# Pool maps moved to a score-bank pair, and FFN squares queued behind the copies of a finished head pair, in a hybrid decoder layer on eight cores

## The chip, the cores and the metric

The kernel runs on the 8 NeuronCores of one Trainium2 chip. Each core computes half of one of four sequences, and no core talks to another. The metric is device time in microseconds of the slowest core. Executions fall into a fast state and a slow one, in which the cores of a die have a clearly lower granted TensorE clock (0.921 to 0.935 on cores 4 to 7 in the slow run of the changed kernel, 0.990 to 0.993 on the others); only fast executions are compared here. "Granted clock" is the share of full TensorE clock that the profile records.

Two kernels are compared, "before" and "the changed kernel". Time before: 1625.96 us (median of 3, 1623.55 to 1628.05).

## The reference, cut to what matters

The layer mixes tokens in three ways from one normalised input, projects, and runs a squared-ReLU MLP.

```python
proj = rmsnorm(x, g_mix) @ w_in                 # q, k, v | u (pooling) | qm (memory queries)
y_attn = dilated_window_attention(...)          # 8 heads of 64, three dilations merged
d = causal_multiscale_pool(u)                   # trailing means of 2/4/8/16 tokens, minus the token
y_pool = einsum('bsgc,gce->bsge', d, w_pool) * pool_scale      # the "pool maps"
y_mem = cross_attention(qm, memory)             # 4 heads
x = x + concat(y_attn, y_pool, y_mem) @ w_out
a = relu(rmsnorm(x, g_ffn) @ w_ff1)
x = x + (a * a) @ w_ff2                         # the "squares"
return rmsnorm(x, g_final)
```

## The kernel before

A core works through tiles of 512 tokens: four halo tiles (only keys, values and pooling margin) and eight own tiles. While the FFN of tile j runs as 64 TensorE groups of 8 matmuls each, the attention of tile j+1 is slipped in between the groups. The groups are FF1 half 0 (positions 0 to 15), FF2 half 0 (16 to 31), FF1 half 1 (32 to 47), FF2 half 1 (48 to 63). Work for between the groups is a list of (position, function).

PSUM is the memory that the matmuls write to. The kernel uses eight banks of it: two "mm" banks in turn for projections and FFN, two score pairs `sc` of two banks each, two banks `ob` for the attention output. In the listings below, `val` is what VectorE copies out of `ob`, `rt` what ScalarE's relu leaves for the square.

```python
mm  = [psum(f"mm{i}", [128, 512], F32) for i in range(2)]
scb = [psum(f"sc{i}", [128, 2, 512], F32) for i in range(2)]
ob  = [psum(f"ob{i}", [128, 512], F32) for i in range(2)]
rt  = [sb(f"rt{i}", [128, 16 + TOK], F32) for i in range(2)]   # relu results (and pooling sums)

def run(groups, side):
    side = sorted(side, key=lambda t: t[0])
    p = 0
    for s, g in enumerate(groups):
        while p < len(side) and side[p][0] <= s:
            side[p][1](); p += 1
        g()
    ...

def front(bt):      # scores of one batch for two heads -> sc pair; exp on ACT -> P; mask product on DVE
    ...
def back(bt):       # P times V -> ob[0], ob[1]; the first batch of a head pair overwrites ob
    ...
    if bt["post"] is None:
        return
    ch = bt["post"]                       # last batch of a head pair: take ob out
    for hh in range(2):
        lo, o2 = 64 * hh, 64 - 64 * hh
        T.op("act", ... den[lo:lo+64] = Ln(ob[hh][o2:o2+64]))
        T.op("dve", ... val[lo:lo+64] = copy(ob[hh][lo:lo+64]))
    T.op("act", ... den = Exp(-den))
    T.op("pool", ... yT[:, ch] = val * den)

def maps(ch):       # one pool map: one matmul into an mm bank, one scaled copy on ACT
    m_, bm_ = next_mm()
    mm_ops(m_[:].rearrange("p (r c) -> p r c", r=4), bm_,
           [(wpool[:, ch, :], dT[:, ch, :].rearrange("p (c r) -> p r c", r=4), [b_wp, b_dT])])
    T.op("act", ... yT[:, 4 + ch, :] = m_ * csm_t[:, 1 + ch:2 + ch])

def ff1(f_):        # 8 matmuls -> mm bank; relu on ACT -> rt; square on DVE -> aT
    def f():
        ...
        mm_ops(m_[:], bm_, [... for k in range(8)])
        r_, br_ = R[cnt["rt"] % len(R)]; cnt["rt"] += 1
        T.op("act", ... r_ = Relu(m_))
        def finish():
            ...
            T.op("dve", ... aT[:, f_ % 16, :] = r_ * r_)
        ...                                # (cut: the last tile keeps four of them back)
        finish()

# the schedule of tile j+1 beside the FFN of tile j
side += att_side(j + 1, 1.875, -4 if first else 0)
pst = pool_steps(j + 1)                    # 11 pooling steps, then the two maps
side += [(17 + i, f) for i, f in enumerate(pst[:-2])] + [(36.5, pst[-2]), (38.5, pst[-1])]
a2 = stage_A(j + 2)                        # RMS norm of tile j+2: squares, statistics, norms
side += ln_side(a2, 6.2, 2, 33.5, 35.2, 1.2)
```

The softmax here doesn't subtract the row's maximum and nothing guards it: scores larger than these inputs give would overflow.

Of the kernel before, what the change touches and what calls it, by code (L numbers as in the profile page):

```python
# [107 lines left out]
def build_nc(n_own=NOWN, races=False):  # L108
# [20 lines left out]
    with ExitStack() as es:  # L129
# [442 lines left out]
        def att_batches(j):  # L572
# [40 lines left out]
                        post=pr if dl == 4 else None))  # L613
            return batches

        def front(bt):
            si, pi = cnt["sc"] % 2, cnt["P"] % NPB
            cnt["sc"] += 1
            cnt["P"] += 1
            s_, bs_, P_, bP_ = scb[si], b_sc[si], Pbuf[pi], b_P[pi]  # L620
            n = len(bt["qk"])
            for i, (sec, l, r) in enumerate(bt["qk"]):
                for hh in range(2):
                    o2 = s_[:, hh, :] if sec is None else s_[:, hh, sec * 128:(sec + 1) * 128]
                    lo = 64 * hh
                    rr = r[lo:lo + 64]
                    if len(rr.shape) == 3:
                        o2 = o2.rearrange("p (a b) -> p a b", a=rr.shape[1])
                    T.op("pe", lambda: nc.tensor.matmul(o2, lhsT=l[lo:lo + 64], rhs=rr, start=True, stop=True),  # L629
                         reads=bt["qk_reads"], writes=[bs_], mark=(i == n - 1 and hh == 1))  # L630
            T.op("act", lambda: nc.scalar.activation(out=P_[:], in_=s_[:], func=AF.Exp, scale=0.125),  # L631
                 reads=[bs_], writes=[bP_])
            if bt["mask"] is not None:
                m, a = bt["mask"]
                Pv = P_[:].rearrange("p h (a q) -> p h a q", a=a)
                T.op("dve", lambda: nc.vector.tensor_tensor(out=Pv, in0=Pv, in1=m, op=ALU.mult),  # L636
                     reads=[bP_, b_E, b_E16], writes=[bP_])
            bt["P"] = (P_, bP_)

        def back(bt):  # L640
            P_, bP_ = bt["P"]
            n = len(bt["pv"])
            for hh in range(2):
                v0 = bt["v0"] + 64 * hh
                for i, (sec, l, oo) in enumerate(bt["pv"]):
                    if sec is None:
                        r_, o_ = P_[:, hh, :], ob[hh][:]
                    else:
                        r_ = P_[:, hh, sec * 128:(sec + 1) * 128]
                        o_ = ob[hh][:].rearrange("p (r c) -> p r c", r=4)[:, oo[0], oo[1]]  # L650
                        r_ = r_.rearrange("p (a b) -> p a b", a=o_.shape[1])
                    T.op("pe", lambda: nc.tensor.matmul(o_, lhsT=l[:, v0:v0 + 128], rhs=r_,  # L652
                                                        start=(bt["first"] and i == 0),
                                                        stop=(bt["last"] and i == n - 1), skip_group_check=True),
                         reads=bt["pv_reads"] + [bP_], writes=[b_ob[hh]], mark=(i == n - 1))
            if bt["post"] is None:
                return
            ch = bt["post"]
            for hh in range(2):
                lo, o2 = 64 * hh, 64 - 64 * hh  # L660
                T.op("act", lambda: nc.scalar.activation(out=den[lo:lo + 64, :], in_=ob[hh][o2:o2 + 64, :], func=AF.Ln),  # L661
                     reads=[b_ob[hh]], writes=[b_den[hh]])
                T.op("dve", lambda: nc.vector.tensor_copy(out=val[lo:lo + 64, :], in_=ob[hh][lo:lo + 64, :]),  # L663
                     reads=[b_ob[hh]], writes=[b_val[hh]])
            T.op("act", lambda: nc.scalar.activation(out=den[:], in_=den[:], func=AF.Exp, scale=-1.0),
                 reads=b_den, writes=b_den)
            T.op("pool", lambda: nc.gpsimd.tensor_tensor(out=yT[:, ch, :], in0=val[:], in1=den[:], op=ALU.mult),  # L667
                 reads=b_den + b_val, writes=[b_yT[ch]])


        def pool_steps(j):
            first_own = (j == NHALO)
            b_serial = Buf("serial")
            W = 16 + TOK
            S1, S2 = rt
            b_S1, b_S2 = b_rt
            ops = []

            def add(out, in0, in1, rd, wr):
                e = "pool" if first_own else "dve"  # L680
                ops.append(lambda: T.op(e, lambda: T.eng[e].tensor_tensor(out=out, in0=in0, in1=in1, op=ALU.add),
                                        reads=rd, writes=wr + ([b_serial] if first_own else [])))

            for ch in range(2):
                Uc = U[:, ch, :]
                add(S1[:, 1:W], Uc[:, 1:W], Uc[:, 0:W - 1], [b_U], [b_S1])
                if ch == 0:
                    add(S2[64:128, 3:W], S1[64:128, 3:W], S1[64:128, 1:W - 2], [b_S1], [b_S2])
                else:
                    add(S2[:, 3:W], S1[:, 3:W], S1[:, 1:W - 2], [b_S1], [b_S2])  # L690
                    add(S1[:, 7:W], S2[:, 7:W], S2[:, 3:W - 4], [b_S2], [b_S1])
                    add(S2[64:128, 15:W], S1[64:128, 15:W], S1[64:128, 7:W - 8], [b_S1], [b_S2])
                halves = ((S1, b_S1, 0), (S2, b_S2, 64))
                if first_own:
                    for s_, bs_, p0 in halves:
                        ops.append(lambda s_=s_, bs_=bs_, p0=p0, ch=ch: T.op(
                            "pool", lambda: nc.gpsimd.tensor_tensor(out=s_[p0:p0 + 64, 16:32], in0=s_[p0:p0 + 64, 16:32],
                                                                   in1=cpc_t[p0:p0 + 64, ch, :], op=ALU.mult),
                            reads=[b_g], writes=[bs_, b_serial]))
                inv = csm_t[:, 3 + ch:4 + ch]  # L700
                for s_, bs_, p0 in halves:
                    ops.append(lambda s_=s_, bs_=bs_, p0=p0, ch=ch, Uc=Uc, inv=inv: T.op(
                        "dve", lambda: nc.vector.scalar_tensor_tensor(out=dT[p0:p0 + 64, ch, :], in0=s_[p0:p0 + 64, 16:W],
                                                                      scalar=inv[p0:p0 + 64, :], in1=Uc[p0:p0 + 64, 16:W],
                                                                      op0=ALU.mult, op1=ALU.subtract),
                        reads=[bs_, b_U, b_g], writes=[b_dT]))
            ops.append(u_margin)

            def maps(ch):
                m_, bm_ = next_mm()  # L710
                mm_ops(m_[:].rearrange("p (r c) -> p r c", r=4), bm_,
                       [(wpool[:, ch, :], dT[:, ch, :].rearrange("p (c r) -> p r c", r=4), [b_wp, b_dT])])
                T.op("act", lambda: nc.scalar.activation(out=yT[:, 4 + ch, :], in_=m_[:], func=AF.Copy,
                                                         scale=csm_t[:, 1 + ch:2 + ch]),
                     reads=[bm_, b_g], writes=[b_yT[4 + ch]])

            ops += [lambda: maps(0), lambda: maps(1)]
            return ops

        def u_margin():  # L720
# [26 lines left out]
        def stage_K(j, late=None):  # L747
# [9 lines left out]
            def ff1(f_):  # L757
                def f():
# [19 lines left out]
                    if late is not None and f_ < 4:  # L778
                        st.setdefault("finish", []).append(finish)
                    else:  # L780
                        for g in st.pop("finish", []):
                            g()
                        finish()
                    if f_ % 4 == 3:
                        ring_issue()
                return f
# [30 lines left out]
# [5 lines that stand above are left out]
                while p < len(side) and side[p][0] <= s:  # L822
                    side[p][1]()
                    p += 1
                g()
            while p < len(side):
                side[p][1]()
                p += 1
# [130 lines left out]
        for j in range(NHALO, NT):  # L959
# [26 lines left out]
            if not last:  # L986
                side += att_side(j + 1, 1.875, -4 if first else 0)
                pst = pool_steps(j + 1)
                side += [(17 + i, f) for i, f in enumerate(pst[:-2])] + [(36.5, pst[-2]), (38.5, pst[-1])]
                if j + 2 < NT:  # L990
                    a2 = stage_A(j + 2)
                    side += ln_side(a2, 6.2, 2, 33.5, 35.2, 1.2)
                side += [(44, lambda j=j: load_x("pool", (j + 1) % 2, xr[j + 1 - NHALO]))]
# [128 lines left out]
```

## Time and profile before

| | before |
|---|---|
| time, median of 3 | 1625.96 us |
| span of the profiled execution, slowest core | 1638.0 us |
| TensorE / VectorE / ScalarE busy | 95% / 58% / 44% |
| tile period, fifth to seventh interval | 183.72, 183.68, 182.17 us |

The last row is worked out from the trace: the time from the first output-projection matmul of one own tile to that of the next. There are seven such intervals. The last three are the same on all eight cores within 0.04 us. The first four vary between cores by 3 to 19 us, because of loads and the granted clock.

The head of the profile page, the slowest core (engine, busy us, share of the span, instructions; PE is TensorE's matmuls, PEld its weight loads, DVE VectorE, ACT ScalarE, POOL GpSimd):

```profile
span 1638.0 us, 27926 instructions; the slowest of 8 cores (1605.7 to 1638.0 us)
...
PE 1558.9 (95%) x9722; PEld 755.0 (46%) x9722; DVE 944.4 (58%) x1378; ACT 722.9 (44%) x1085; POOL 161.1 (10%) x219
...
PEclk9998788999999999999999999999999999999998
```

TensorE (PE) is the bottleneck, so only its gaps matter. The clock row (one digit for each fortieth of the span, in tenths) has a 7 and three 8s in slices four to seven; core 3 was throttled between about 100 and 300 us (granted clock 0.80 from 150 to 250 us, where core 7 has 1.00), which makes it longer than most cores. So the table of TensorE's waits (who waited for whom: us in total, times, longest) is shown for core 3 and for core 7. Core 3:

```profile
PE mm L350 <- DVE acc L381: 24.2, 3, 17.7
PE mm L350 <- ACT rt L768: 12.7, 10, 4.6
PE ob L652 <- DVE val L663: 11.0, 29, 0.9
```

The same table of core 7, the two lines on the copies and on `rt`:

```profile
PE ob L652 <- DVE val L663: 12.2, 30, 1.4
PE mm L350 <- ACT rt L768: 8.3, 9, 4.2
```

The waits on `rt` and on `val` are what the change is about. The single waits behind such a sum are called idle entries below: idle time that the profile lists before an instruction, in square brackets, with what ended it. The timeline of core 3 shows one of each (columns: start us, duration us, engine, line, operation, out<-in, count, idle of that engine before and what ended it). First the copies, with TensorE, ScalarE (ACT) and VectorE (DVE) together, near the end of the second FF1 half:

```profile
1092.53 0.61 PE L652 MATMUL ob<-P,Vd 128*128 128x128 bf16 x8
...
1092.97 1.89 PE L350 MATMUL mm<-h2T,ring 128*128 128x512 bf16 x8
1093.52 1.21 ACT L661 ACTIVATE den<-ob 64x512 f32<-64x512 f32 x2
1093.60 0.69 DVE L775 TENSOR_TENSOR aT<-rt 128x512 bf16<-128x512 f32 x1 [1.03 <-ACT rt L768]
1094.32 1.41 DVE L663 COPY val<-ob 64x512 f32<-64x512 f32 x2
...
1095.15 0.38 PE L652 MATMUL ob<-P,Vd 128*128 128x128 bf16 x4 [0.29 <-DVE val L663]
...
1095.88 0.38 PE L652 MATMUL ob<-P,Vd 128*128 128x128 bf16 x4 [0.34 <-DVE val L663]
...
1096.10 1.89 PE L350 MATMUL mm<-aT,ring 128*128 128x512 bf16 x8
```

VectorE was idle for 1.03 us, then did a square that had been waiting for its relu, and only then the two copies, although `ob` was complete (ScalarE read it at 1093.52). TensorE had to wait before each half of the next head pair. Next the two pool maps, with TensorE and, of ScalarE, the two relus that free a bank:

```profile
1069.23 0.61 PE L350 MATMUL mm<-dT,wpool 128*128 128x512 bf16 x1
1069.60 0.60 ACT L768 ACTIVATE rt<-mm 128x512 f32<-128x512 f32 x1 [1.63 <-DVE hT L411]
1069.66 0.63 PE L652 MATMUL ob<-P,Vd 128*128 128x128 bf16 x8
1070.34 1.89 PE L350 MATMUL mm<-h2T,ring 128*128 128x512 bf16 x8
1072.16 0.64 PE L629 MATMUL sc<-Q,KT 64*128 64x128 bf16 x16
1072.73 1.90 PE L350 MATMUL mm<-h2T,ring 128*128 128x512 bf16 x8
1074.47 0.61 PE L350 MATMUL mm<-dT,wpool 128*128 128x512 bf16 x1
1074.84 0.60 ACT L768 ACTIVATE rt<-mm 128x512 f32<-128x512 f32 x1
1075.58 1.89 PE L350 MATMUL mm<-h2T,ring 128*128 128x512 bf16 x8 [0.50 <-ACT rt L768]
1077.30 0.61 PE L652 MATMUL ob<-P,Vd 128*128 128x128 bf16 x8
1077.75 1.89 PE L350 MATMUL mm<-h2T,ring 128*128 128x512 bf16 x8
```

After the second map the next FF1 group needs the mm bank of the group before the map, whose relu has just been issued: 0.50 us of idle.

### The profile page before, as it was taken

How to read it: one execution, taken by the hardware profiler on the slowest of the kernel's cores; microseconds unless marked ns; L12 is line 12 of the kernel's file. 1: busy time of each engine (PE TensorE's matmuls, PEld its weight loads, DVE VectorE, ACT ScalarE, POOL GpSimd, SP SyncE). 2: the span in 40 equal slices, each digit the busy share in tenths (PEclk: the TensorE clock that was granted, in tenths of full speed). 3: DMA queues.
4: the chain of work that ended last, by engine and by line, in shares of the span. 5: the costliest groups of instructions: out<-in, count | busy, mean ns of one | idle time of the engine just before them, and what ended most of it. 6: DMA issues, size and time to landing. Idle time of an engine off the chain costs nothing.

```text
span 1638.0 us, 27926 instructions; the slowest of 8 cores (1605.7 to 1638.0 us)
## 1 busy us (share of the span) xinstructions
PE 1558.9 (95%) x9722; PEld 755.0 (46%) x9722; DVE 944.4 (58%) x1378; ACT 722.9 (44%) x1085; POOL 161.1 (10%) x219
## 2 busy tenths in 40 slices
PE   4989899989899999999999999999999999999996
PEld 1434534544355444544445544544455544544442
DVE  4665555556366555666465565666475565545654
ACT  3645554442445436453354436353354435354222
POOL 3121110010101001000100010000100000000001
PEclk9998788999999999999999999999999999999998
DMA  9767446686978668574765665343833463343542
GB/s 243 178 213 230 116 68 133 110 177 201 219 162 191 182 215 229 149 202 164 234 191 138 217 208 191 129 155 130 295 116 143 155 228 121 128 172 138 186 151 101
DMA packets 43241, 282.93 MB, mean 173 GB/s; under 512 B 5344, under 2 KB 7520, under 8 KB 10976
## 3 DMA queue, kind: packets, MB, share of 16 engines
q0 software_dynamic: 17952, 121.45, 31.0%
q1 hardware_dynamic: 24576, 158.64, 27.7%
q8 instruction: 81, 1.33, 0.3%
q10 hardware_dynamic: 576, 1.05, 0.2%
q14 instruction: 56, 0.46, 0.1%
HBM read 286.69 MB, written 46.92 MB: 204 GB/s over the span
## 4 chain that ended last, share of the span: by engine, by line
PE 85%; DMA 5%; DVE 4%; ACT 3%; issue 3%; POOL 1%; ACTq 0%; DVEq 0%; SPq 0%; POOLq 0%
PE mm L350 73%; PE ob L652 6%; PE sc L629 4%; DMA X<-xh 2%; DMA ring<-wall 2%; PE sc L350 2%; DVE val L663 1%; ACT P L631 1%; ACT rt L768 1%; DVE acc L381 1%; ACT Vd L355 0%; DMA cpc_t<-cpc 0%; DVE aT L775 0%; POOL Vd L268 0%; DVE P L636 0%
## 5 line engine op out<-in xcount | busy, mean ns | idle before, releaser
L350 PE MATMUL mm<-h2T,ring 128*128 128x512 bf16 x2192 | 517.6, 386 | 15.2 <-ACT rt L768 12.7
L350 PE MATMUL mm<-aT,ring 128*128 128x512 bf16 x2048 | 472.0, 382 | 5.4 <-DMA ring<-wall 3.8
L631 ACT ACTIVATE P<-sc 128x1024 bf16<-128x1024 f32 x256 | 247.5, 1023 | 209.2 <-PE sc L629 208.4
L350 PEld LDWEIGHTS mm<-h2T,ring 128*128 128x128 bf16 x2192 | 206.5, 99 | 265.5 <-issue 60.5
L775 DVE TENSOR_TENSOR aT<-rt 128x512 bf16<-128x512 f32 x232 | 184.1, 793 | 214.5 <-ACT rt L768 212.3
L350 PEld LDWEIGHTS mm<-aT,ring 128*128 128x128 bf16 x2048 | 193.4, 98 | 220.7 <-issue 15.5
L768 ACT ACTIVATE rt<-mm 128x512 f32<-128x512 f32 x232 | 138.3, 596 | 240.2 <-PE mm L350 185.9
L636 DVE TENSOR_TENSOR P<-P,E 128x1024 bf16<-128x1024 bf16 x224 | 154.2, 694 | 135.1 <-ACT P L631 134.1
L371 ACT ACTIVATE sq<-X 128x512 f32<-128x512 f32 x196 | 121.8, 627 | 182.6 <-DVE X L801 109.8
L652 PE MATMUL ob<-P,Vd 128*128 128x128 bf16 x1792 | 140.9, 223 | 12.3 <-DVE val L663 11.0
L652 PEld LDWEIGHTS ob<-P,Vd 128*128 128x128 bf16 x1792 | 119.6, 100 | 70.4 <-issue 30.6
L350 PE MATMUL mm<-hT,ring 128*128 128x512 bf16 x672 | 148.2, 380 | 2.7 <-ACT acc L387 2.2
L801 DVE TENSOR_TENSOR X<-X,mm 128x512 f32<-128x512 f32 x128 | 87.7, 685 | 103.4 <-PE mm L350 101.2
L381 DVE TENSOR_TENSOR acc<-acc,sq 128x512 f32<-128x512 f32 x144 | 105.2, 731 | 43.5 <-ACT sq L371 41.8
L667 POOL TENSOR_TENSOR yT<-val,den 128x512 bf16<-128x512 f32 x48 | 63.4, 1321 | 656.7 <-DVE val L663 335.5
L350 PE MATMUL mm<-yT,ring 128*128 128x512 bf16 x512 | 117.2, 389 | 2.2 <-POOL yT L667 1.7
L350 PEld LDWEIGHTS mm<-hT,ring 128*128 128x128 bf16 x672 | 65.4, 98 | 85.5 <-issue 9.5
L350 PEld LDWEIGHTS mm<-yT,ring 128*128 128x128 bf16 x512 | 50.5, 100 | 69.3 <-issue 19.1
L411 DVE SCALAR_TENSOR_TENSOR h2T<-X,gc,acc 128x512 bf16<-128x512 f32 x80 | 56.0, 745 | 35.3 <-ACT acc L389 30.3
L629 PE MATMUL sc<-Q,KT 64*128 64x128 bf16 x1792 | 73.0, 222 | 1.3 <-ACT P L631 1.3
L629 PEld LDWEIGHTS sc<-Q,KT 64*128 64x128 bf16 x1792 | 54.0, 107 | 41.6 <-issue 38.1
L661 ACT ACTIVATE den<-ob 64x512 f32<-64x512 f32 x96 | 56.7, 591 | 30.2 <-PE ob L652 28.3
(108 smaller groups left out, 939.3 us busy)
## 6 DMA issues: line engine op xcount, KB each, us to landing
ring<-wscratch SPq DMA_DIRECT2D x123, 1024.0 KB, 5.9
ring<-wall POOLq DMA_DIRECT2D x48, 1024.0 KB, 9.8
X<-xh POOLq DMA_DIRECT2D x22, 1024.0 KB, 16.4
wscratch<-ring SPq DMA_DIRECT2D x21, 1024.0 KB, 4.7
X<-xr POOLq DMA_DIRECT2D x16, 1024.0 KB, 10.4
out<-X POOLq DMA_DIRECT2D x14, 1024.0 KB, 9.4
vscratch<-Vd POOLq DMA_DIRECT2D x24, 192.0 KB, 7.1
Vd<-vscratch POOLq DMA_DIRECT2D x6, 768.0 KB, 9.8
```

The lines of the kernel that those rows point to most:

```text
L350: T.op("pe", lambda: nc.tensor.matmul(out_ap, lhsT=l, rhs=r, start=(i == 0), stop=(i == n - 1)), reads=rd, writes=[b_out], mark=(i == n - 1))
L371: T.op("act", lambda: nc.scalar.activation(out=s_, in_=self.x3[:, k, :], func=AF.Square), reads=[self.b_x[k]], writes=[bs_])
L381: T.op("dve", lambda: nc.vector.tensor_tensor(out=self.acc, in0=self.acc, in1=s_, op=ALU.add), reads=[bs_], writes=self.b_acc)
L629: T.op("pe", lambda: nc.tensor.matmul(o2, lhsT=l[lo:lo + 64], rhs=rr, start=True, stop=True), reads=bt["qk_reads"], writes=[bs_], mark=(i ...
L631: T.op("act", lambda: nc.scalar.activation(out=P_[:], in_=s_[:], func=AF.Exp, scale=0.125), reads=[bs_], writes=[bP_])
L636: T.op("dve", lambda: nc.vector.tensor_tensor(out=Pv, in0=Pv, in1=m, op=ALU.mult), reads=[bP_, b_E, b_E16], writes=[bP_])
L652: T.op("pe", lambda: nc.tensor.matmul(o_, lhsT=l[:, v0:v0 + 128], rhs=r_, start=(bt["first"] and i == 0), stop=(bt["last"] and i == n - 1) ...
L661: T.op("act", lambda: nc.scalar.activation(out=den[lo:lo + 64, :], in_=ob[hh][o2:o2 + 64, :], func=AF.Ln), reads=[b_ob[hh]], writes=[b_den ...
L667: T.op("pool", lambda: nc.gpsimd.tensor_tensor(out=yT[:, ch, :], in0=val[:], in1=den[:], op=ALU.mult), reads=b_den + b_val, writes=[b_yT[ch]])
L768: T.op("act", lambda: nc.scalar.activation(out=r_, in_=m_[:], func=AF.Relu), reads=[bm_], writes=br_)
L775: T.op("dve", lambda: nc.vector.tensor_tensor(out=aT[:, a_, :], in0=r_, in1=r_, op=ALU.mult), reads=br_, writes=[b_aT[a_]])
L801: T.op("dve", lambda: nc.vector.tensor_tensor(out=xi[:, d, :], in0=xi[:, d, :], in1=m_[:], op=ALU.add), reads=[bm_], writes=[bxi[d]])
```

## The change

The intent is to take both waits away. The two maps go together into one score pair, so that they no longer take turns with FF1 in the mm banks. The square of an FF1 group is kept in a list and put into VectorE's queue at the next score batch, after the copies of a finished head pair, after an `ob` batch that finishes none, or before the next group, whichever comes first.

```diff
+        deferred = []
+
+        def flush():
+            while deferred:
+                deferred.pop(0)()
+
         def front(bt):
+            flush()
             ...
         def back(bt):
             ...
             if bt["post"] is None:
+                flush()
                 return
             ...                      # Ln on ACT and copy on DVE for both heads
+            flush()
             T.op("act", ... den = Exp(-den))
@@
-            def maps(ch):
-                m_, bm_ = next_mm()
-                mm_ops(m_[:].rearrange("p (r c) -> p r c", r=4), bm_, ...)
-                T.op("act", ... yT[:, 4 + ch, :] = m_ * csm_t[:, 1 + ch:2 + ch])
-            ops += [lambda: maps(0), lambda: maps(1)]
+            def maps():
+                si = cnt["sc"] % 2
+                cnt["sc"] += 1
+                for ch in range(2):
+                    mm_ops(scb[si][:, ch, :].rearrange("p (r c) -> p r c", r=4), b_sc[si], ...)
+                for ch in range(2):
+                    T.op("act", ... yT[:, 4 + ch, :] = scb[si][:, ch, :] * csm_t[:, 1 + ch:2 + ch])
+            ops.append(maps)
@@ ff1
-                        for g in st.pop("finish", []):
-                            g()
-                        finish()
+                        deferred.extend(st.pop("finish", []))
+                        deferred.append(finish)
@@ run
                     side[p][1]()
                     p += 1
+                flush()
                 g()
@@
-                side += [(17 + i, f) for i, f in enumerate(pst[:-2])] + [(36.5, pst[-2]), (38.5, pst[-1])]
+                side += [(17 + i, f) for i, f in enumerate(pst[:-1])] + [(36.5, pst[-1])]
```

More of the change, by code (lines that the diff above doesn't have):

```diff
@@ L707, in pool_steps @@
             ops.append(u_margin)
-            def maps(ch):
-                m_, bm_ = next_mm()
-                mm_ops(m_[:].rearrange("p (r c) -> p r c", r=4), bm_,
-                       [(wpool[:, ch, :], dT[:, ch, :].rearrange("p (c r) -> p r c", r=4), [b_wp, b_dT])])
-                T.op("act", lambda: nc.scalar.activation(out=yT[:, 4 + ch, :], in_=m_[:], func=AF.Copy,
-                                                         scale=csm_t[:, 1 + ch:2 + ch]),
-                     reads=[bm_, b_g], writes=[b_yT[4 + ch]])
-            ops += [lambda: maps(0), lambda: maps(1)]
+            def maps():
+                si = cnt["sc"] % 2
+                cnt["sc"] += 1
+                for ch in range(2):
+                    mm_ops(scb[si][:, ch, :].rearrange("p (r c) -> p r c", r=4), b_sc[si],
+                           [(wpool[:, ch, :], dT[:, ch, :].rearrange("p (c r) -> p r c", r=4), [b_wp, b_dT])])
+                for ch in range(2):
+                    T.op("act", lambda: nc.scalar.activation(out=yT[:, 4 + ch, :], in_=scb[si][:, ch, :], func=AF.Copy,
+                                                             scale=csm_t[:, 1 + ch:2 + ch]),
+                         reads=[b_sc[si], b_g], writes=[b_yT[4 + ch]])
+            ops.append(maps)
             return ops
```

## The prediction

> **What bounds the kernel.** TensorE: on the profiled slowest core (span 1638.0 us) it is busy 95%, VectorE 58%, ScalarE 44%; the chain of waits is 85% TensorE. So the change is worth only the TensorE gaps it closes. The table of waits gives 24.2 us for the RMS sums (3 times), 12.7 us on the rectified values `rt` (10), 11.0 us on the copies `val` (29).
>
> **The gaps aimed at** (timeline):
> - `val`. After a head pair, the next pair's first matmuls overwrite `ob` and wait for two copies of 0.69 us. In each of seven tiles one such place is in the second FF1 half. There a square (0.69 us), itself waiting for its relu, stands ahead of the copies: near 1093 us ScalarE starts to read `ob` at 1093.52, the copies start at 1094.32. TensorE idles 0.28 + 0.34 us (0.83 + 0.34 us in the first tile). The other steady place (near 1035, 0.41 + 0.34 us) is in an FF2 half, where a `dT` step, an RMS add and a residual add stand ahead, no square; two more (159, 185 us) have no FFN beside them. These stay.
> - `rt`. The second pool map takes one of two mm banks, so the next FF1 group waits for a relu just issued: 0.50 us per tile, seven times (for example at 1075.58). The first map shows no wait. The large `rt` waits (4.57, 2.62, 2.00 us) are ScalarE held by a square that waits for the load `X<-xh`; these stay.
>
> **What the change does.** No arithmetic goes or comes: 16 map matmuls (0.61 us) and 16 scaled copies (0.68 us) stay. The maps go into a score pair, which the next scores but one need only after a whole FF1 group (1.89 us), enough for their copies (1.37 us). Squares move behind the copies, and also behind VectorE steps placed between groups (one norm of 0.75 us, sometimes two, or an RMS add of 0.69 us), as the built order shows. A relu needs its buffer two groups later, over 3.8 us, so I expect no steady new wait. The Trainium skill, "PSUM — Partial Sum Buffer", section "Engine vs sequencer instructions", says VectorE and ScalarE queues are strict FIFO; the copies held behind a square at 1093 us agree.
>
> **On the critical path.** `val`: 1.17 + 6 x 0.62 = 4.9 us. Maps: 7 x 0.50 = 3.5 us. First own tile: perhaps 0.4 us. Against this about 0.8 us of new small waits or longer weight waits in the first tiles. Net, as an estimate from these durations, 8 us of 1626 (0.5%).
>
> **Predicted: 1618 us, range 1609 to 1627.** Chances: faster by over 2%: 0.02; within 2%: 0.96; slower by over 2%: 0.02.
>
> **What would show it.** TensorE's wait on `val` falls from 11.0 to about 6 us, the rest in FF2 halves and the first attention; its wait on `rt` falls by 3.5 us, with no 0.50 us entries. No new TensorE wait on score banks or yT. Busy times stay within 1%. Two map matmuls stand together, with no idle after them.
>
> **What would make it wrong.** The late squares make relu wait for `rt` (ScalarE on `aT` above 7 us) and TensorE for mm banks: then near 1626. The granted clock: cores 2 and 3 have 0.80 between 150 and 250 us where the others have 1.00, and core 3 is 32 us longer than the shortest; which cores get this, and how long, moves the slowest core by more than the change. Loads in the early tiles (DMA share above 0.9 near 400 us) may swallow 1 to 2 us.

## The result, and the profile after

The changed kernel took 1611.68 us (median of 4 runs, one of them slow at 1694.67; the median of the three fast ones is 1610.86); before took 1625.7 us beside it. The ratio is 0.9911, 95% interval 0.9892 to 0.9931. A ratio is the mean time of one kernel's fast runs over that of the other's of the same rounds, so not quite the ratio of the medians quoted. Run again with the experiments below, the same kernel gave 1610.25 against 1621.79 us, ratio 0.9932 (0.9917 to 0.9947). By the medians of fast runs it is 11.5 to 14.8 us faster and clear of noise.

The head of the page of the changed kernel:

```profile
span 1609.8 us, 27719 instructions; the slowest of 8 cores (1597.8 to 1609.8 us)
...
PE 1512.6 (94%) x9556; PEld 749.1 (47%) x9722; DVE 942.0 (59%) x1378; ACT 723.3 (45%) x1085; POOL 161.2 (10%) x219
```

This core's trace (core 4) lacks 166 matmul records, 9556 against 9722, which lowers TensorE's busy time and strews small false gaps; core 3 is complete, so it is read from here on. Its table of waits:

```profile
PE mm L350 <- DVE acc L381: 23.2, 3, 16.6
PE ob L659 <- DVE val L671: 7.1, 16, 1.1
PE mm L350 <- ACT rt L781: 6.2, 2, 3.9
```

Against core 7 of before, also at full clock, the wait on the copies fell from 12.2 to 7.1 us (30 to 16 times). The wait on `rt` is left with two entries; the seven of 0.50 us are gone. The timeline of core 3 at the places that answer to those of before, first the copies:

```profile
1056.15 0.61 PE L659 MATMUL ob<-P,Vd 128*128 128x128 bf16 x8
...
1056.59 1.89 PE L350 MATMUL mm<-h2T,ring 128*128 128x512 bf16 x8
1056.78 1.41 DVE L671 COPY val<-ob 64x512 f32<-64x512 f32 x2 [0.59 <-PE ob L659]
...
1058.22 0.69 DVE L788 TENSOR_TENSOR aT<-rt 128x512 bf16<-128x512 f32 x1
1058.32 0.66 PE L659 MATMUL ob<-P,Vd 128*128 128x128 bf16 x8
...
1058.82 1.46 PE L350 MATMUL mm<-aT,ring 128*128 128x512 bf16 x6
```

The copies start 0.63 us after the last `ob` batch began (1.79 us before the change), and the square comes after them. From the FF1 group to the group after the next `ob` batch TensorE needs 2.23 us (1056.59 to 1058.82), before 3.13 us (1092.97 to 1096.10): 0.90 us less, although the idle entries that vanished say 0.29 + 0.34 = 0.63. The maps, TensorE only:

```profile
1031.99 1.89 PE L350 MATMUL mm<-h2T,ring 128*128 128x512 bf16 x8
1033.71 1.06 PE L350 MATMUL sc<-dT,wpool 128*128 128x512 bf16 x2
1034.60 0.63 PE L659 MATMUL ob<-P,Vd 128*128 128x128 bf16 x8
1035.06 1.89 PE L350 MATMUL mm<-h2T,ring 128*128 128x512 bf16 x8
```

The two maps take 0.89 us together. The `ob` batch after them is followed after 0.46 us, and there is no idle entry.

| tile period, us (mean of eight cores) | 5th | 6th | 7th |
|---|---|---|---|
| before | 183.72 | 183.68 | 182.17 |
| changed | 181.92 | 182.06 | 180.40 |
| difference | 1.80 | 1.62 | 1.77 |

The entries promised 0.50 + 0.62 = 1.12 us per tile. The experiments ask where the other 0.6 us come from.

### The profile page after: what moved, and what is told of

The parts are those of the page before. It is cut to its first block, busy times and chain, and to the rows that moved or that the text cites. A ratio compares the mean times of both kernels' runs of the same rounds, so it can differ in the third digit from the quotient of the medians.

```text
span 1609.8 us, 27719 instructions; the slowest of 8 cores (1597.8 to 1609.8 us)
## 1 busy us (share of the span) xinstructions
PE 1512.6 (94%) x9556; PEld 749.1 (47%) x9722; DVE 942.0 (59%) x1378; ACT 723.3 (45%) x1085; POOL 161.2 (10%) x219
## 3 DMA queue, kind: packets, MB, share of 16 engines
q10 hardware_dynamic: 576, 1.05, 0.2%
## 4 chain that ended last, share of the span: by engine, by line
PE 86%; DMA 5%; issue 3%; DVE 3%; ACT 2%; POOL 1%; ACTq 0%; DVEq 0%; SPq 0%; POOLq 0%
PE mm L350 73%; PE ob L659 6%; PE sc L636 4%; DMA X<-xh 2%; PE sc L350 2%; DMA ring<-wall 2%; DVE val L671 1%; DVE acc L381 1%; ACT Vd L355 1%; DMA cpc_t<-cpc 0%; ACT P L638 0%; POOL Vd L268 0%; DVE X L407 0%; DVE X L411 0%; ACT den L669 0%
## 5 line engine op out<-in xcount | busy, mean ns | idle before, releaser
L350 PE MATMUL mm<-h2T,ring 128*128 128x512 bf16 x2123 | 494.8, 381 | 23.6 <-ACT rt L781 12.4
L350 PE MATMUL mm<-aT,ring 128*128 128x512 bf16 x1987 | 457.8, 380 | 14.7 <-issue 6.9
L659 PE MATMUL ob<-P,Vd 128*128 128x128 bf16 x1792 | 137.5, 219 | 8.2 <-DVE val L671 7.0
L671 DVE COPY val<-ob 64x512 f32<-64x512 f32 x96 | 66.0, 687 | 31.3 <-PE ob L659 29.6
```

The lines of the kernel that those rows point to most:

```text
L350: T.op("pe", lambda: nc.tensor.matmul(out_ap, lhsT=l, rhs=r, start=(i == 0), stop=(i == n - 1)), reads=rd, writes=[b_out], mark=(i == n - 1))
L659: T.op("pe", lambda: nc.tensor.matmul(o_, lhsT=l[:, v0:v0 + 128], rhs=r_, start=(bt["first"] and i == 0), stop=(bt["last"] and i == n - 1) ...
L671: T.op("dve", lambda: nc.vector.tensor_copy(out=val[lo:lo + 64, :], in_=ob[hh][lo:lo + 64, :]), reads=[b_ob[hh]], writes=[b_val[hh]])
```

## The experiments

Theory A: a stall of TensorE costs more than its idle entry. The profile counts idle from the recorded end of a matmul. A 128x512 matmul is recorded as 0.379 us long, but in a stream the next one starts 0.216 us after it (eight take 1.89 us: 7 x 0.216 + 0.379). So a matmul may start 0.163 us late before any idle shows, and every entry understates its stall by that much. A 128x128 matmul of the `ob` batches gives the same difference (recorded as 0.219 us, 0.056 us from start to start). The Trainium skill, "Perfetto Trace Analysis", section "Per-engine timelines", says that the end of a TensorE instruction is estimated, not observed; the two pairs of numbers above fit that, but would also fit matmuls that truly overlap. Theory A needs only the difference. Rival B: the entries are the whole cost, and the rest comes from elsewhere. Rival C: the squares' new place behind norms and RMS adds (VectorE's sums of squares for the next norm), which the change also brings, gives part of it.

All eight runs were correct. The first four shared one chip and the runs of before; the last four another.

### maps_only: the maps alone

```diff
-            def maps(ch): ... next_mm() ...        # as in before
+            def maps(): ... scb[si] ...            # as in the change; squares as in before
```

> Before with only the pool maps moved into a score pair; squares as before. Measure: the tile period (from the first output-projection matmul of one tile to that of the next) of the fifth full tile, at full clock: before 183.72, after 181.92 us. Theory A (an idle entry of TensorE understates a stall by about 0.16 us, since a matmul is recorded 0.38 us long and issued every 0.22 us, and the first map has a stall of 0.22 us that no entry shows): 0.66 + 0.22 = 0.88 us less, period 182.8; time about 6 us less, ratio 0.996. Rival B (the entries are the whole cost, the rest of the gain comes from elsewhere): 0.50 us less, period 183.2; ratio 0.998.

Measured: periods 182.85, 182.82, 181.30 us, so 0.87 us less per tile in each; 1618.9 against 1623.09 us by the medians of fast runs, ratio 0.9963 (0.9934 to 0.9992). Theory A's 0.88 holds, B's 0.50 does not. The sum is 0.50 + 0.16 at the second map and 0.22 at the first, the stall without an entry.

### squares_only: the deferred squares alone

```diff
+        deferred / flush() in front, back, ff1 and run   # as in the change
             def maps(ch): ... next_mm() ...              # as in before
```

> Before with only the deferred squares; maps as before in mm banks at two places. Theory A: the two val stalls of the second FF1 half go, 0.28 + 0.34 us of entries plus twice 0.16, so 0.95 us less: period 182.8; time about 7 us less, ratio 0.9955. Rival B: 0.62 us less, period 183.1. Rival C (the squares' new place behind norms and RMS adds is what helps): period below 182.6. The two parts should add up to the whole change (1.80 us) if they are independent.

Measured: 182.79, 182.78, 181.29 us, so 0.93, 0.90 and 0.88 us less; 1617.04 against 1623.09 us by the medians of fast runs (one of six was slow), ratio 0.9958 (0.9927 to 0.999). Again A (0.95), not B (0.62), and nothing is left for C in these tiles. In the fifth interval the parts add up to the whole: 0.87 + 0.93 = 1.80 us. In the sixth they promise 1.76 and the change has 1.62.

### maps_score_apart: the bank without the joint place

```diff
             def maps(ch):
-                m_, bm_ = next_mm()
+                si = cnt["sc"] % 2
+                cnt["sc"] += 1
+                m_, bm_ = scb[si][:, 0, :], b_sc[si]       # still at 36.5 and 38.5
```

> Before with the maps in score banks but at their two old places, one score pair each: is it the bank or the joint place that helps? If the bank: period 182.8 as for the maps alone. If the joint place: 183.7, as before. The waits table should have no 0.50 us entries on rt if it is the bank.

Measured (one look): 182.85, 182.82, 181.30 us, the same as the maps together, and three entries on `rt` on core 7, where before has nine. The bank is the cause; once the maps are in score banks, putting them side by side adds nothing.

### maps_mm_together: the joint place without the bank

```diff
-                side += ... [(36.5, pst[-2]), (38.5, pst[-1])]
+                side += ... [(36.5, pst[-2]), (36.5, pst[-1])]
```

> Before with both maps at the first place, still in mm banks. If the bank is what matters: the second map waits for the relu just issued and the next FF1 group for the first map's copy, so period 183.6 to 184.6. If the joint place is what matters: 182.8.

Measured (one look): 183.51, 183.48, 181.96 us. That is 0.21 us less than before and 0.09 us below the range expected. The timeline of core 1 shows the stall moved to the second map:

```profile
1039.20 0.61 PE L350 MATMUL mm<-dT,wpool 128*128 128x512 bf16 x1
...
1040.31 0.61 PE L350 MATMUL mm<-dT,wpool 128*128 128x512 bf16 x1 [0.50 <-ACT rt L768]
...
1040.74 0.63 PE L652 MATMUL ob<-P,Vd 128*128 128x128 bf16 x8
...
1041.21 1.89 PE L350 MATMUL mm<-h2T,ring 128*128 128x512 bf16 x8
```

The second map starts 1.11 us after the first instead of 0.45, which is 0.66 us of stall under an entry of 0.50. The `ob` batch is followed after 0.47 us, so the hidden 0.22 us of the first map is gone, and it is what the period lost. The expectation had missed that.

### changed_again: the changed kernel as an anchor

> The changed kernel unaltered, once more, beside the next ones: ratio 0.991 as before; tile periods 181.92, 182.05, 180.41 for the last three full tiles.

Measured: 1610.25 against 1621.79 us, ratio 0.9932 (0.9917 to 0.9947), a smaller gain than the 0.9911 expected, with overlapping intervals; periods 181.92, 182.05, 180.40 us as expected. The mean granted clock over all cores of the fast runs was 0.991 for this kernel and 0.992 for before, so the clock did not give the gain.

### squares_pass_copies_only: squares held back for the copies alone

```diff
@@ run, on top of the change
                 while p < len(side) and side[p][0] <= s:
+                    if not getattr(side[p][1], "holds", False):
+                        flush()
                     side[p][1]()
@@ att_side: the function of a back with a finished head pair gets holds = True
```

> The changed kernel, but a square is held back only past the copies of a finished head pair; it goes ahead of norms and RMS adds again, as in before. Theory A (only the copies matter): period of the fifth full tile 181.92, as the changed kernel. Rival C (passing norms and adds gives part of the gain): above 182.1. The 0.14 us that the sixth tile lost against the sum of the two parts (182.05 against 181.91) may go, if it comes from those passes.

Measured: 181.96, 181.92, 180.40 us (the one fast run took 1608.79 us). The fifth period is within 0.04 us of the changed kernel's, so C falls. The sixth got its 0.14 us back: letting squares fall behind norms and RMS adds cost that much in one tile and gave nothing there. The edit has a side effect in the first own tile: on every core the waits of 0.83 and 0.34 us on the copies are back (the total on `val` is 8.2 us in 18 entries, not 7.1 in 16), so C is ruled out by the last three intervals, not for that tile.

### pool_steps_moved: the copies of the first FF2 half

Of the 7.1 us left on the copies, half is in the first FF2 half (0.38 + 0.34 us in each of five tiles), where pooling steps and an RMS add stand ahead of them. The timeline of core 3 of the changed kernel:

```profile
997.99 0.75 DVE L712 SCALAR_TENSOR_TENSOR dT<-rt,csm_t,U 64x512 bf16<-64x512 f32 x1
998.03 1.21 ACT L669 ACTIVATE den<-ob 64x512 f32<-64x512 f32 x2 [1.60 <-PE ob L659]
998.78 0.69 DVE L381 TENSOR_TENSOR acc<-acc,sq 128x512 f32<-128x512 f32 x1
...
999.39 1.40 DVE L671 COPY val<-ob 64x512 f32<-64x512 f32 x2
...
1000.21 0.38 PE L659 MATMUL ob<-P,Vd 128*128 128x128 bf16 x4 [0.38 <-DVE val L671]
...
1000.93 0.38 PE L659 MATMUL ob<-P,Vd 128*128 128x128 bf16 x4 [0.34 <-DVE val L671]
```

```diff
-                side += [(17 + i, f) for i, f in enumerate(pst[:-1])] + [(36.5, pst[-1])]
+                side += [(p_, f) for p_, f in zip([16.2, 16.6, 17, 17.4, 22, 23, 24, 25, 26, 27, 28], pst[:-1])] + [(36.5, pst[-1])]
-                    side += ln_side(a2, 6.2, 2, 33.5, 35.2, 1.2)
+                    side += ln_side(a2, 6.2, 1.85, 33.5, 35.2, 1.2)
```

> The changed kernel with the pooling steps of VectorE placed so that no dT step, and one RMS add fewer, stands ahead of the copies of the head pair that ends in the first FF2 half. The waits left there show 0.38 + 0.34 us. Theory A: stalls cost 0.16 more each, so 1.05 us less per tile: period 180.9 (fifth tile), time about 7 us less than the changed kernel. Rival B (the entry is the cost): 0.72 less, 181.2. TensorE's wait on val falls from 7 to about 3 us (the first attention and little else).

Measured: 180.88, 180.88, 179.97 us. The fifth period fell by 1.04 us, A's 1.05 and not B's 0.72. The seventh fell by 0.43 us; there the changed kernel has one entry at this place, 0.28 us, so that A gives 0.44 and B 0.28. The copies now start with ScalarE's reading of `ob` (core 3):

```profile
1000.93 1.21 ACT L669 ACTIVATE den<-ob 64x512 f32<-64x512 f32 x2 [1.60 <-PE ob L659]
1000.95 1.41 DVE L671 COPY val<-ob 64x512 f32<-64x512 f32 x2
...
1002.56 0.61 PE L659 MATMUL ob<-P,Vd 128*128 128x128 bf16 x8
```

The wait on `val` fell to 4.4 us in 6 entries (3 us were expected). On every core two of the six are new: 1.17 and 0.34 us in the first own tile, where the changed kernel has one entry of 0.25. The time, 1606.84 against 1621.79 us (ratio 0.9911, 0.9894 to 0.9929), is 3.4 us below the changed kernel's median in the same rounds, half of the 7 us expected: the last three intervals give 2.6 us together, and in the profiled executions the first four were together no shorter (727.3 against 726.7 us in the mean of the cores). What the stalls gave there was lost again: by A the new wait takes about 1.4 us of it, and the first interval is 1.3 us longer (171.09 against 169.76, with 5 to 6 us between cores). The rest went to loads as it seems; that was not tested by itself.

### rms_squares_later: no square waiting for a load at the head of ScalarE's queue

In early tiles the largest wait of TensorE inside the FFN is ScalarE held by an RMS square whose input is still being loaded. Core 4 of the changed kernel:

```profile
423.64 0.63 ACT L371 ACTIVATE sq<-X 128x512 f32<-128x512 f32 x1 [6.21 <-DMA X<-xh]
...
427.23 2.34 PE L350 MATMUL mm<-h2T,ring 128*128 128x512 bf16 x5 [6.06 <-ACT rt L781]
```

From 425.6 to 432.3 us the profile's granted clock is 0.50, before and after it 1.00. The five matmuls of the second line take 2.34 us, where eight take 1.89 at full clock: the stall costs more than its length. The Trainium skill, "TensorE: Matmul & The Clock Gate", section "What's actually happening", says that the array falls to half clock after an idle window of about 3.4 us; the idle of 6.06 us and the clock of 0.50 agree with it.

```diff
@@ on top of pool_steps_moved
-                    side += ln_side(a2, 6.2, 1.85, 33.5, 35.2, 1.2)
+                    for k, at in enumerate((9.4, 11.2, 13.2, 15.2, 17.2, 19.1, 20.9, 22.9)):
+                        side.append((at, lambda k=k, a2=a2: a2.square(k)))
+                    side += [(33.5, a2.stat)] + [(35.2 + 1.2 * k, lambda k=k, a2=a2: a2.norm(k)) for k in range(8)]
```

> The same as the pool steps moved, and the squares of the next RMS norm start 3.2 groups later, so that ScalarE is not held by a square waiting for the load X<-xh. In the changed kernel this holds TensorE 6.06, 5.07 and 1.00 us in the second to fourth tile, and the granted clock then drops to 0.5 for 3.4 us. If that is right, those periods fall from 187 to 190, 185 to 189 and 182 to 184 us to 181 to 183 us: 8 to 14 us of time beyond the run before it. If loads limit these tiles otherwise, the wait only moves to weights and the gain is under 4 us.

Measured: 1603.61 against 1621.79 us by the medians of fast runs (one of six was slow), ratio 0.9886 (0.987 to 0.9902). The second to fourth periods are 187.62, 184.39 and 181.02 us in the mean of the cores, against 187.28, 186.36 and 182.60 in the run before it. The gain over that run is 3.2 us by the medians of fast runs, so the other branch of the expectation came true: the wait moved to weights. At the same place of core 4:

```profile
432.54 1.86 PE L350 MATMUL mm<-h2T,ring 128*128 128x512 bf16 x4 [4.24 <-DMA ring<-wall]
```

Its total on weights is now 12.7 us, against 5.1 us in the changed kernel. This version is nevertheless the fastest one run here: 18.2 us below before by the same medians.

## Why the prediction was right, and which of its terms was mis-sized

The time, 1611.68 us, lies inside the stated range of 1609 to 1627, and the class (within 2%) is right. The range also holds the time before, 1625.7 us, so that a time inside it says little about the mechanism: the forecast gain was 8 us, the measured one 11.5 to 14.8. What speaks for the mechanism is the experiments. Point by point:

- **TensorE bounds it, and only its gaps count: shown.** Nothing but queue order and banks changed, and the time moved by the gaps that closed.
- **The square ahead of the copies, once per tile in the second FF1 half: shown.** squares_only removes it alone, and the wait on the copies of core 7 fell from 12.2 to 7.3 us; in the changed kernel it is 7.1, 5.1 less against the 4.9 predicted. The ones in the FF2 half stayed, as predicted, until pool_steps_moved took them away.
- **The second map's mm bank: shown.** maps_score_apart and maps_mm_together tell the bank from the place.
- **"The first map shows no wait": wrong.** It showed no entry, but cost 0.22 us, visible only as a longer distance between two starts (0.68 against 0.45 us).
- **The mis-sized terms are "`val`: 1.17 + 6 x 0.62 = 4.9 us" and "Maps: 7 x 0.50 = 3.5 us".** Their mechanism was right and their sizes were read from idle entries. Measured one by one they are 0.90 us (mean of 0.93, 0.90 and 0.88) and 0.87 us per tile. Over seven tiles, as an estimate from these figures, that is 12.4 us in place of 8.4. The prediction's two small terms, 0.4 us gained in the first own tile and 0.8 us lost in early tiles, were not measured by themselves. The mean over all cores of the fast runs fell by 11.7 us in the second comparison (1613.8 to 1602.1), close to it.
- **"No steady new wait": nearly right.** ScalarE's wait for squares rose from 7.7 to 10.4 us on core 7 and from 7.0 to 12.1 us on core 3, above the 7 us that the prediction named as its alarm, but TensorE lost only 0.14 us in one tile; squares_pass_copies_only ties that to the squares that fall behind norms and adds. The trace shows where: at 1210.14 us on core 3 of the changed kernel an FF1 group starts 0.14 us after a relu that ends late, since ScalarE had begun the relu of an earlier group 0.48 us after its matmuls, and 0.20 us in squares_pass_copies_only. What held that earlier relu is not settled.
- **The clock:** it did not move the second comparison (0.991 against 0.992). Of the fast runs whose clocks are on record, no core outside the profiled execution of before fell below 0.983; the clocks of before's other runs beside the first result are not on record.
- **Not settled:** how much of the gain the first four intervals carry, where loads move the period by more than 1.8 us from core to core, and whether the first result's 14.8 us or the second's 11.5 us is nearer to the truth. The intervals of the two ratios overlap. Nor was it looked into why the stretch after the last landmark grew by about half a us in the changed kernel (144.5 to 145.5 us, before 143.7 to 144.7).

## What to carry to other kernels

On a TensorE-bound kernel, size a stall by the distance between the starts of two matmul groups, compared with the same pair of groups where nothing waits; the idle entry leaves out the recorded tail of the last matmul, and short stalls leave no entry at all. A repeating period measured between fixed landmarks resolves 0.05 us where the time resolves a few, and shows whether two changes add up. When a PSUM bank is freed by an engine whose records follow its program order, as VectorE's did at 1093 us, put the freeing copy ahead of work that waits for something else, and give small odd matmuls a bank that is not in the tight rotation.

## What the Trainium skill lacked or had wrong

- "Perfetto Trace Analysis", "Per-engine timelines", says that a matmul's end is estimated, but not what follows for gaps: here a stall was 0.16 us longer than its idle entry (0.66 against 0.50 at the pool map), and one of 0.22 us had no entry.
- "TensorE: Matmul & The Clock Gate", "Back-to-back issue gap", gives about 131 ns per matmul as the sustained spacing of weight-load and matmul pairs at 512 columns. Such a stream ran at 216 ns at full clock (eight matmuls in 1.89 us with the last one's 0.379), which is nearer to what the page calls the isolated gap.
- No page says that some cores' traces lack matmul records: 9556 of 9722 on core 4 here, with false gaps of 0.16 us in their place.
